# SwiGLU's result turned by VectorE's block transposes and GpSimd's moves instead of TensorE's transposes, in 13 of 22 blocks

## The chip, the cores and the metric

The kernel runs on one core of one Trainium2 chip. Its time is the device time of one execution in microseconds (us); runs before and after are compared by their medians. Where a row comes from a profile, it is from one profiled execution.

## What is computed

One decoder layer for 256 tokens (`SEQ`) of width 2048: a SwiGLU feed-forward layer (half step), a token mixer, and a second SwiGLU layer, each between two RMS norms and with shift, scale and gate from a conditioning vector `c`. The part that matters here:

```python
def swiglu(h, w_gate, w_up, w_down):
    return (jax.nn.silu(h @ w_gate) * (h @ w_up)) @ w_down

mod = (jax.nn.silu(c) @ w_ada[l] + b_ada[l]).reshape(b_, N_SUBLAYERS, N_MOD, D_MODEL)
x = sublayer(x, 0, ffn(0), 0.5)
x = sublayer(x, 1, mixer, 1.0)
x = sublayer(x, 2, ffn(1), 0.5)
```

`D_FF` is 5632. All inputs are float32, and all weights are read once.

## The kernel before

**Weights.** A weight tile is 256 rows by 512 columns, 512 KB. SyncE's queue (SP) issues one load for it into a buffer of the pool `raw`, which has 8 buffers of 4 KB a partition (L304). ScalarE (ACT) rounds it to `wh` (L315), VectorE (DVE) subtracts to get the rest `wl` (L320), each in one of `NW = 4` buffers, and TensorE (PE) multiplies three times for each product: `wh` with the activation's high part (L338), `wl` with it (L339), `wh` with its low part (L340). A tile takes 12 such multiplications of 512 columns. Loads go out in order; each waits for its buffer, which is free when the subtraction has read the tile that was in it.

**The conditioning vector.** Its products with `w_ada` are made by DVE alone, from buffers of the same pool `raw` (loads L157 and L162, sums L170 and L172). These "side" units are spread between the weight tiles: many in the first feed-forward layer, few in the second.

**Blocks.** The feed-forward width is cut into 11 blocks of 512 for each layer. A block makes gate and up in PSUM, tokens on partitions (`proj_tok`); `swiglu_evac` or `swiglu_sum` makes silu(gate) * up as two tiles `gt` of 128 tokens by 512. The down product needs the result with the feed-forward width on partitions. `to_g` does that: for each half of the block four transposes by TensorE (L542) into one PSUM bank, then `split_act`, which rounds on ACT (L373) and subtracts on DVE (L374) into the slot `g`. Blocks are grouped in "supers": after the gates and ups of a super its down products run. In layer 0 the supers have 4, 4 and 3 blocks (the blocks of the first have parts of the work done earlier), in layer 1 they have 4, 4 and 3.

**Order.** The evacuation is a generator in the list `pending`; after every weight tile `pump` lets it go one step. `swiglu_evac` takes its first step behind the first weight tile of the next block; both halves of `to_g` come two and three tiles later. `flush` runs what is left at the end of a block. The order of instructions on each engine, and which buffer of a pool a tile gets, are settled when the kernel is compiled.

Of the kernel before, what the change touches and what calls it, by code (L numbers as in the profile page):

```python
# [8 lines left out]
F32 = mybir.dt.float32  # L9
# [5 lines left out]
P = 128  # L15
D = 2048
S = 256
NT = S // P
# [14 lines left out]
def tile_layer(  # L33
# [6 lines left out]
    nc = tc.nc  # L40
# [14 lines left out]
    rawp = ctx.enter_context(tc.tile_pool(name="rawp", bufs=8))  # L55
# [9 lines left out]
    def nm(s):  # L65
        uid[0] += 1
        return f"{s}_{uid[0]}"

    def ps():
        return psp.tile([P, 512], F32, tag="ps", name=nm("ps"))  # L70

    def t2(shape=(P, 512), dtype=F32):
        return tp.tile(list(shape), dtype, tag="t2", name=nm("t2"))
# [203 lines left out]
    pending = []  # L277
# [17 lines left out]
    def flush():  # L295
        while pending:
            pump()
# [39 lines left out]
    def mm3(o, lh, ll, rh, rl, start, stop):  # L337
        nc.tensor.matmul(o, lh, rh, start=start, stop=False, skip_group_check=True)  # L338
        nc.tensor.matmul(o, lh, rl, start=False, stop=False, skip_group_check=True)  # L339
        nc.tensor.matmul(o, ll, rh, start=False, stop=stop, skip_group_check=True)  # L340

    def hold(src, segs, c0, nw):

        n = sum(nk for _, nk, _ in segs) // 2
        slots = [Slot((P, 2, 2, 512), F32R) for _ in range(n - nw)]
        return list(w_tiles(src, segs, c0, [None] * min(n, nw) + [s_.t for s_ in slots])), slots
# [14 lines left out]
    def proj_tok(src, c0, begun=None, w=512, segs=FULL, banks=None, first=0):  # L361

        if begun is not None:
            banks, segs = begun[0], FULL[begun[1]:]
        banks = banks or [ps(), ps()]
        last = segs[-1][0] + segs[-1][1] - 1
        for k, wh, wl in w_tiles(src, segs, c0, w=w):
            for t in range(NT):
                tok_mm(k, wh, wl, t, banks[t][:, 0:w], first, last)
        return banks  # L370

    def split_act(dh, dl, src):
        act = nc.scalar.copy(dh, src)  # L373
        return nc.vector.tensor_tensor(out=dl, in0=src, in1=dh.bitcast(F32), op=ALU.subtract), act  # L374


    def parts():

        p = small((P, 8), "parts")
        nc.gpsimd.memset(p[:, 3:4], EPS)  # L380
        return p

    def sumsq(p, q, src):
        junk = t2()
        nc.scalar.activation(junk, src, AF.Square, scale=float(D) ** -0.5, accum_out=p[:, q + q // 3:q + q // 3 + 1])  # L385
# [147 lines left out]
        return banks, 2  # L533


    def to_g(g, gts):
        for i in range(2):
            pg = ps()
            for j in range(2):
                for t in range(NT):  # L540
                    m = 2 * i + j
                    nc.tensor.transpose(pg[:, j * S + t * P:j * S + (t + 1) * P], gts[t][:, m * P:(m + 1) * P], ident)  # L542
            split_act(g.t[:, 0, 2 * i:2 * i + 2, :], g.t[:, 1, 2 * i:2 * i + 2, :],
                      pg.rearrange("p (k s) -> p k s", s=S))
            yield

    def swiglu_evac(g, gb, ub):
        gts = []
        for t in range(NT):
            sg, gt = t2(), t2()  # L550
            nc.scalar.activation(sg, gb[t], AF.Silu)
            nc.vector.tensor_tensor(out=gt, in0=sg, in1=ub[t], op=ALU.mult)
            gts.append(gt)
        yield
        yield
        yield from to_g(g, gts)

    def swiglu_sum(gb, ub, part):

        pv = part.t.rearrange("p k s -> p (k s)")  # L560
        gts = []
        for t in range(NT):
            sg, gt = t2(), t2()
            nc.vector.tensor_tensor(out=sg, in0=pv[:, t * 512:(t + 1) * 512], in1=gb[t], op=ALU.add)
            nc.scalar.activation(sg, sg, AF.Silu)
            nc.vector.tensor_tensor(out=gt, in0=pv[:, 1024 + t * 512:1024 + (t + 1) * 512], in1=ub[t], op=ALU.add)
            nc.vector.tensor_tensor(out=gt, in0=sg, in1=gt, op=ALU.mult)
            gts.append(gt)
        part.free()
        g = Slot((P, 2, 4, S), F32R)  # L570

        def rest():
            yield
            yield
            yield from to_g(g, gts)

        pending.append(rest())
        return g

    def ffn(idx, supers, begun, xin, nxt, nxt_src=None, nxt_c0=None, nxt_w=512):  # L580

        y = None
        yp = [parts() for _ in range(NT)]

        def evac_y(si, q, t, bank):
            ys = y[t].t[:, q * 512:(q + 1) * 512]
            if si == 0:
                nc.scalar.copy(ys, bank)
            else:
                nc.vector.tensor_tensor(out=ys, in0=ys, in1=bank, op=ALU.add)  # L590
            if si == len(supers) - 1:
                sumsq(yp[t], q, ys)

        for si, blocks in enumerate(supers):
            gs = []
            n = len(blocks)
            for b, segs, part, banks in blocks:
                if si == 0 and begun is not None and not gs:
                    gb = proj_tok(w_ff_gate[idx], b * FB, begun)
                    ub = proj_tok(w_ff_up[idx], b * FB)  # L600
                elif part is not None:
                    gb = proj_tok(w_ff_gate[idx], b * FB, segs=segs, first=segs[0][0])
                    ub = proj_tok(w_ff_up[idx], b * FB, segs=segs, first=segs[0][0])
                    flush()
                    gs.append(swiglu_sum(gb, ub, part))
                    continue
                else:
                    gb = proj_tok(w_ff_gate[idx], b * FB, segs=segs, banks=banks and banks[0])
                    ub = proj_tok(w_ff_up[idx], b * FB, segs=segs, banks=banks and banks[1])
                flush()  # L610
                gs.append(Slot((P, 2, 4, S), F32R))
                pending.append(swiglu_evac(gs[-1], gb, ub))
            if y is None:
                y = [Slot((P, D)) for _ in range(NT)] if xin[0].__class__ is Half else [Half(t) for t in range(NT)]
            rows = [(4 * i, 4, 4 * b[0]) for i, b in enumerate(blocks)]

            def mms(k, wh, wl, t):
                g = gs[k // 4].t
                mm3(banks[t], g[:, 0, k % 4, t * P:(t + 1) * P], g[:, 1, k % 4, t * P:(t + 1) * P],
                    wh, wl, k == 0, k == 4 * n - 1)  # L620

            for q in range(4):
                banks = [ps(), ps()]
                if si == len(supers) - 1 and q == 2:
                    for s_ in xin:
                        s_.t
                if si == len(supers) - 1 and q == 3:
                    flush()
                    if side[0] is not None:
                        side[0].drain()  # L630
                    early = early_w(nxt_src, nxt_c0, nxt_w)
                    kept, slots = hold(w_ff_down[idx], rows, q * 512, NW if nxt is None else 3)

                    def last_mm(t):
                        for k, wh, wl in kept:
                            mms(k, wh, wl, t)

                    return boundary(last_mm, lambda t: evac_y(si, q, t, banks[t]), lambda t: times_gg(y, t, q), xin, y, yp, slots + gs,
                                    early, 1, nxt, nxt_src, nxt_c0, nxt_w)
                else:  # L640
                    for k, wh, wl in w_tiles(w_ff_down[idx], rows, q * 512):
                        for t in range(NT):
                            mms(k, wh, wl, t)
                    for t in range(NT):
                        later(evac_y, si, q, t, banks[t])
                        if si == len(supers) - 1:
                            later(times_gg, y, t, q)
            if si < len(supers) - 1:
                for g in gs:
                    g.free()  # L650
# [68 lines left out]
    for bs, n in (((0, 1, 2, 3, 4), 1), ((5, 6), 2), ((7,), 3)):  # L719
        first.until(n - 1)  # L720
        for b in bs:
            part = Slot((P, 8, S))
# [5 lines left out]
    banks = [proj_tok(gate_up[u], 8 * FB, segs=FULL[:3]) for u in range(2)]  # L728
# [26 lines left out]
    blocks = [(4718, 410), (4308, 410), (3896, 412), (3484, 412), (G0, 412)]  # L755
# [61 lines left out]
    for i, (c0, w) in enumerate(blocks):  # L817
        banks = proj_tok(w_in, c0, begun if i == 0 else None, w)
# [147 lines left out]
    for i in range(2):  # L966
        banks = proj_t(w_in, i * 512)
# [72 lines left out]
    for i in range(2):  # L1040
        banks = proj_tok(w_in, O0 + i * 512)
# [44 lines left out]
    for q in range(4):  # L1086
        banks = b0 if q == 0 else [ps(), ps()]
# [55 lines left out]
```

## Time and profile before

| what | us |
|---|---|
| median of 3 runs | 1872.24 |
| lowest and highest | 1871.8 and 1872.76 |
| the profiled execution | 1872.83 |
| its span, first to last instruction | 1870.8 |

The profiled execution is 0.6 us above the median; 2.0 us of it lie outside its span. In the rows, PE is TensorE, PEld its weight loads, POOL is GpSimd, SPq is SyncE's queue. L followed by a number is a line of the kernel. A row of a group gives the count, the busy time and the mean of one instruction; what stands behind the last bar is the idle time just before them and who ended it. Shapes are partitions x elements.

### The profile page before, as it was taken

To read this page: it belongs to the slowest core of one execution; us is meant where nothing else is said; L and a number is where in the kernel's file an instruction comes from. 1 tells how busy PE (TensorE), PEld (TensorE's weight loads), DVE (VectorE), ACT (ScalarE), POOL (GpSimd) and SP (SyncE) were. 2 spreads that over 40 slices of the span, in tenths; PEclk is the share of its full clock that TensorE was granted. 3 is DMA by queue.
4 is the path that set the end of the run, shared out by engine and by line. 5 is a ranking of instruction groups with operands and counts; after the bars stand their busy time and mean duration, and the time that the engine had idled before them with its cause. 6 is when DMAs were issued, how large, how long until landed. Compare 5 with 4: busy or idle time off the path is not lost.

```text
span 1870.8 us, 23057 instructions
## 1 busy us (share of the span) xinstructions
PE 1823.0 (97%) x8501; PEld 1523.7 (81%) x8501; DVE 1365.0 (73%) x1479; ACT 853.6 (46%) x1058; POOL 22.5 (1%) x42
## 2 busy tenths in 40 slices
PE   3999999999999999999999999999999999999998
PEld 2888888888888888799988887888888888888886
DVE  6888798788987888868898987555556555556455
ACT  3555444444443444655545446444444444334443
POOL 1000000000000000000000000000000000000000
PEclk9999999999999999999999999999999999999999
DMA  9999889999899999578689994776677776677662
GB/s 346 346 359 342 314 293 318 319 307 322 294 331 323 340 306 334 188 240 278 218 288 306 358 342 141 221 223 213 228 228 221 221 223 214 219 228 220 190 190 91
DMA packets 232617, 499.82 MB, mean 267 GB/s; under 512 B 16828, under 2 KB 28332, under 8 KB 231992
## 3 DMA queue, kind: packets, MB, share of 16 engines
q1 hardware_dynamic: 232504, 498.36, 79.9%
q8 instruction: 66, 1.08, 0.2%
q14 instruction: 47, 0.39, 0.1%
HBM read 496.19 MB, written 2.10 MB: 266 GB/s over the span
## 4 chain that ended last, share of the span: by engine, by line
PE 86%; issue 8%; DVE 3%; DMA 2%; POOL 1%; ACT 0%; DVEq 0%; POOLq 0%; ACTq 0%; SPq 0%
PE ps L338 28%; PE ps L339 28%; PE ps L340 28%; DVE acc L172 2%; PE ps L542 1%; DVE wl L320 1%; DMA raw<-in_w_ada_dram 1%; DMA raw<-in_w_ff_up_dram 0%; POOL rstd L391 0%; DMA raw<-in_w_ff_gate_dram 0%; DMA xt<-in_x_dram 0%; PE ps L197 0%; PE ps L930 0%; ACT wh L315 0%; POOL brs L808 0%
## 5 line engine op out<-in xcount | busy, mean ns | idle before, releaser
L320 DVE TENSOR_TENSOR wl<-raw,wh 128x1024 fp32r<-128x1024 f32 (+2 forms) x635 | 766.1, 1210 | 450.3 <-ACT wh L315 449.3
L315 ACT CAST wh<-raw 128x1024 fp32r<-128x1024 f32 (+2 forms) x637 | 662.6, 1043 | 864.1 <-PE ps L340 737.0
L338 PE MATMUL ps<-wh,hh 128*128 128x512 f32 (+2 forms) x1680 | 650.3, 390 | 1.5 <-ACT hh L373 1.5
L339 PE MATMUL ps<-wl,hh 128*128 128x512 f32 (+2 forms) x1680 | 649.3, 387 | 1.2 <-DVE wl L320 1.2
L340 PE MATMUL ps<-wh,hl 128*128 128x512 f32 (+2 forms) x1680 | 649.1, 386 | 0.0
L339 PEld LDWEIGHTS ps<-wl,hh 128*128 128x128 f32 x1680 | 316.5, 188 | 61.9 <-DVE wl L320 2.7
L340 PEld LDWEIGHTS ps<-wh,hl 128*128 128x128 f32 x1680 | 316.1, 188 | 60.5
L338 PEld LDWEIGHTS ps<-wh,hh 128*128 128x128 f32 x1680 | 315.9, 188 | 60.1 <-ACT hh L373 1.7
L172 DVE SCALAR_TENSOR_TENSOR acc<-raw,cs,acc 128x1024 f32<-128x1024 f32 x270 | 345.1, 1278 | 0.8 <-DVE parts L389 0.4
L338 PE MATMUL ps<-wh,big 128*128 128x512 f32 x804 | 314.6, 392 | 0.0
L339 PE MATMUL ps<-wl,big 128*128 128x512 f32 x804 | 313.1, 389 | 0.2 <-DVE wl L320 0.2
L340 PE MATMUL ps<-wh,big 128*128 128x512 f32 x804 | 313.1, 389 | 0.0
L339 PEld LDWEIGHTS ps<-wl,big 128*128 128x128 f32 x804 | 151.0, 188 | 31.8 <-DVE wl L320 1.0
L340 PEld LDWEIGHTS ps<-wh,big 128*128 128x128 f32 x804 | 150.9, 188 | 31.7
L338 PEld LDWEIGHTS ps<-wh,big 128*128 128x128 f32 x804 | 150.9, 188 | 30.6
L338 PE MATMUL ps<-hh,wh 128*128 128x256 f32 x128 | 37.6, 293 | 0.0
L680 ACT COPY big<-ps 128x512 f32<-128x512 f32 x32 | 18.7, 589 | 40.8 <-PE ps L340 39.5
L374 DVE TENSOR_TENSOR big<-ps,big 128x512 fp32r<-128x512 f32 x52 | 35.5, 683 | 1.3 <-ACT big L373 1.2
L340 PE MATMUL ps<-hh,wl 128*128 128x256 f32 x128 | 36.2, 283 | 0.0
L339 PE MATMUL ps<-hl,wh 128*128 128x256 f32 x128 | 36.2, 283 | 0.0
L373 ACT CAST big<-ps 128x512 fp32r<-128x512 f32 x52 | 30.1, 578 | 0.0
L385 ACT ACTIVATE t<-xt 128x512 f32<-128x512 f32 x32 | 20.0, 626 | 17.7 <-DVE xt L590 9.6
(194 smaller groups left out, 751.4 us busy)
## 6 DMA issues: line engine op xcount, KB each, us to landing
raw<-in_w_ada_dram SPq DMA_DIRECT2D x224, 512.0 KB, 5.3
raw<-in_w_ff_gate_dram SPq DMA_DIRECT2D x176, 512.0 KB, 4.5
raw<-in_w_ff_up_dram SPq DMA_DIRECT2D x176, 512.0 KB, 4.5
raw<-in_w_ff_down_dram SPq DMA_DIRECT2D x176, 512.0 KB, 5.1
raw<-in_w_ada_dram SPq DMA_DIRECT2D x128, 256.0 KB, 5.5
raw<-in_w_in_dram SPq DMA_DIRECT2D x48, 512.0 KB, 5.1
raw<-in_w_out_dram SPq DMA_DIRECT2D x32, 512.0 KB
raw<-in_w_in_dram SPq DMA_DIRECT2D x24, 412.0 KB, 4.8
```

The source lines that it names most:

```text
L172: ins = nc.vector.scalar_tensor_tensor(a, raw[:, j, :, :], cs[:, k:k + 1], a, op0=ALU.mult, op1=ALU.add)
L315: behind(nc.scalar.copy(wh, rawv), floor[1])
L320: last_split[0] = nc.vector.tensor_tensor(out=wl, in0=rawv, in1=wh.bitcast(F32), op=ALU.subtract)
L338: nc.tensor.matmul(o, lh, rh, start=start, stop=False, skip_group_check=True)
L339: nc.tensor.matmul(o, lh, rl, start=False, stop=False, skip_group_check=True)
L340: nc.tensor.matmul(o, ll, rh, start=False, stop=stop, skip_group_check=True)
L373: act = nc.scalar.copy(dh, src)
L374: return nc.vector.tensor_tensor(out=dl, in0=src, in1=dh.bitcast(F32), op=ALU.subtract), act
L385: nc.scalar.activation(junk, src, AF.Square, scale=float(D) ** -0.5, accum_out=p[:, q + q // 3:q + q // 3 + 1])
L542: nc.tensor.transpose(pg[:, j * S + t * P:j * S + (t + 1) * P], gts[t][:, m * P:(m + 1) * P], ident)
L680: nc.scalar.copy(part.t.rearrange("p k s -> p (k s)")[:, u * 1024 + i * 512:u * 1024 + (i + 1) * 512], banks[i])
```

## The change

A block takes another way than `to_g` where the next block of its super still multiplies at least 12 of the 16 groups of 128 weight rows, which is 12 to 16 weight tiles for gate and up. These are 3 and 2 blocks of the last two supers of layer 0 and 3, 3 and 2 of layer 1: 13 of 22. In that way VectorE transposes each `gt` in blocks of 32 by 32 into `tr`, GpSimd copies 16 pieces (32 partitions by 256 elements, in runs of 32) to their places in `gf`, and nine weight tiles later `split_act` reads `gf` instead of PSUM. `tr` and `gf` are tiles of the pool `raw`. The other nine blocks go on as before.

```diff
+    def to_g_blocks(g, gts):
+        tr = rawp.tile([P, NT, 4, 4, 32], F32, tag="raw", name=nm("tr"))
+        gf = rawp.tile([P, 4, NT, 4, 32], F32, tag="raw", name=nm("gf"))
+        for t in range(NT):
+            nc.vector.transpose(tr[:, t].rearrange("p m q r -> p (m q r)"), gts[t])
+        for b in range(4):
+            for q in range(4):
+                nc.gpsimd.tensor_copy(gf[q * 32:(q + 1) * 32, :, :, b, :].rearrange("p m t r -> p t m r"),
+                                      tr[b * 32:(b + 1) * 32, :, :, q, :])
+        for _ in range(9):
+            yield
+        for i in range(2):
+            split_act(g.t[:, 0, 2 * i:2 * i + 2, :], g.t[:, 1, 2 * i:2 * i + 2, :],
+                      gf[:, 2 * i:2 * i + 2].rearrange("p m t b r -> p m (t b r)"))
+            yield
...
-    def swiglu_evac(g, gb, ub):
+    def swiglu_evac(g, gb, ub, blocks):
...
         yield
-        yield
-        yield from to_g(g, gts)
-
-    def swiglu_sum(gb, ub, part):
+        if blocks:
+            yield from to_g_blocks(g, gts)
+        else:
+            yield
+            yield from to_g(g, gts)
+
+    def swiglu_sum(gb, ub, part, blocks):
...
         def rest():
             yield
-            yield
-            yield from to_g(g, gts)
+            if blocks:
+                yield from to_g_blocks(g, gts)
+            else:
+                yield
+                yield from to_g(g, gts)
...
-            for b, segs, part, banks in blocks:
+            for i, (b, segs, part, banks) in enumerate(blocks):
+
+                slow = i + 1 < n and sum(nk for _, nk, _ in blocks[i + 1][1]) >= 12
```

## Rows read from the trace of the kernel before

**Rows 1.** The page's first part: busy time, share, instructions of each engine.
```profile
PE 1823.0 (97%) x8501; PEld 1523.7 (81%) x8501; DVE 1365.0 (73%) x1479; ACT 853.6 (46%) x1058; POOL 22.5 (1%) x42
```

**Rows 2.** The page's chain that ended last, shares of the span by line.
```profile
PE ps L338 28%; PE ps L339 28%; PE ps L340 28%; DVE acc L172 2%; PE ps L542 1%; DVE wl L320 1%; DMA raw<-in_w_ada_dram 1%; DMA raw<-in_w_ff_up_dram 0%; POOL rstd L391 0%; DMA raw<-in_w_ff_gate_dram 0%; DMA xt<-in_x_dram 0%; PE ps L197 0%; PE ps L930 0%; ACT wh L315 0%; POOL brs L808 0%
```

**Rows 3.** Waits over the whole span: us in total, times, longest.
```profile
ACT wh L315 <- PE ps L340: 737.0, 460, 3.2
DVE wl L320 <- ACT wh L315: 449.3, 418, 3.8
```

**Rows 4.** Stretches: busy us (instructions) of PE, PEld, DVE, ACT, POOL; clock, DMA share, GB/s.
```profile
405.00:507.00 102.00, 102.00 (x475) 83.94 (x474) 90.04 (x97) 44.12 (x48) 0.00 (x0) 1.00 0.90 310
630.00:720.00 90.00, 90.00 (x413) 74.23 (x412) 73.12 (x69) 38.48 (x41) 0.00 (x0) 1.00 0.93 321
1165.00:1340.00 175.00, 175.00 (x789) 144.85 (x788) 98.12 (x89) 74.91 (x81) 0.00 (x0) 1.00 0.71 221
```

**Rows 5.** Timeline of PE in layer 1: start us, us, instruction.
```profile
1179.73 0.39 PE L338 MATMUL ps<-wh,hh 128*128 128x512 f32 x1
...
1182.45 0.39 PE L338 MATMUL ps<-wh,hh 128*128 128x512 f32 x1
...
1183.13 0.60 PE L542 MATMUL ps<-ident,t 128*128 128x128 f32 x4
...
1186.34 0.60 PE L542 MATMUL ps<-ident,t 128*128 128x128 f32 x4
```

**Rows 6.** Groups by line and shape: DVE's, then ACT's.
```profile
L320 DVE TENSOR_TENSOR wl<-raw,wh 128x1024 fp32r<-128x1024 f32 x597 | 728.0, 1222 | 431.8 <-ACT wh L315 430.9 <-issue 0.3
...
L374 DVE TENSOR_TENSOR big<-ps,big 128x512 fp32r<-128x512 f32 x52 | 35.5, 683 | 1.3 <-ACT big L373 1.2
...
L183 DVE STREAM_TRANSPOSE t<-acc 128x512 f32<-128x512 f32 x22 | 14.6, 692 | 0.1
...
L374 DVE TENSOR_TENSOR hl<-t,hh 128x512 fp32r<-128x512 f32 x14 | 9.3, 686 | 0.1
...
L315 ACT CAST wh<-raw 128x1024 fp32r<-128x1024 f32 x599 | 629.3, 1054 | 829.2 <-PE ps L340 707.0 <-issue 35.6 <-DMA raw<-in_w_ff_gate_dram 26.4
L373 ACT CAST big<-ps 128x512 fp32r<-128x512 f32 x52 | 30.1, 578 | 0.0
...
L373 ACT CAST hh<-t 128x512 fp32r<-128x512 f32 x14 | 8.3, 620 | 0.1
```

**Rows 7.** POOL's groups by line and shape; the last gives min/median/max ns.
```profile
L318 POOL TENSOR_TENSOR wl<-raw,wh 128x1024 fp32r<-128x1024 f32 x2 | 4.7, 2358 | 22.2 <-ACT wh L315 17.8 <-DMA raw<-in_w_ada_dram 4.4
...
L380 POOL MEMSET parts<- 128x1 f32 x12 | 1.1, 98 | 0.6
...
L843 POOL TENSOR_SCALAR_AFFINE_SELECT big<-onesr 128x128 f32<-128x128 f32 x1 | 0.3, 292 | 1.1 <-PE ps L340 1.1
masks.py:197 POOL MEMSET ident<- 128x128 f32 x1 | 0.2, 204 | 0.3 <-POOLq L1130 0.3
...
L391 POOL TENSOR_TENSOR rstd<-parts,nhalf x12: 548/548/1534, 11.2 to 1864.0; 128x1 f32<-128x1 f32 x12
```

**Rows 8.** Timelines of POOL and DVE in the mixer: start us, us, instruction.
```profile
895.75 1.18 POOL L891 TENSOR_SCALAR_AFFINE_SELECT t<-t 128x512 f32<-128x512 f32 x1 [43.31 <-DMA raw<-in_w_in_dram]
907.81 0.64 POOL L891 TENSOR_SCALAR_AFFINE_SELECT t<-t 128x512 f32<-128x512 f32 x1 [10.88 <-DMA raw<-in_w_in_dram]
...
895.74 0.68 DVE L898 TENSOR_TENSOR t<-t,t 128x512 f32<-128x512 f32 x1
...
907.94 1.05 DVE L898 TENSOR_TENSOR t<-t,t 128x512 f32<-128x512 f32 x1
```

**Rows 9.** Timelines of DVE and PE in layer 0: one tile's subtraction, its first use.
```profile
403.68 1.22 DVE L320 TENSOR_TENSOR wl<-raw,wh 128x1024 fp32r<-128x1024 f32 x1
...
408.61 0.40 PE L339 MATMUL ps<-wl,hh 128*128 128x512 f32 x1
```

**Rows 10.** Line L304's loads, 405 to 507 us: issue to landing.
```profile
DMA to landing us min/median/max: 4.3/5.3/6.8
```

More of the change, by code (lines that the diff above doesn't have):

```diff
@@ L604, in ffn @@
                     flush()
-                    gs.append(swiglu_sum(gb, ub, part))
+                    gs.append(swiglu_sum(gb, ub, part, slow))
                     continue
@@ L611, in ffn @@
                 gs.append(Slot((P, 2, 4, S), F32R))
-                pending.append(swiglu_evac(gs[-1], gb, ub))
+                pending.append(swiglu_evac(gs[-1], gb, ub, slow))
             if y is None:
```

## The prediction, made blind

> **What bounds the kernel now.** I read the busy shares first: TensorE is busy 97% of the span, VectorE 73%, ACT 46%, GpSimd 1% [rows 1]. The chain that ended last runs through TensorE's three products with 28% each, and the transposes L542 have 1% of it by themselves [rows 2]. The waits turn it round: ACT's rounding waits for TensorE 460 times, to get a `wh` buffer back, and VectorE's subtraction waits for ACT [rows 3]. So the splitting of weights runs ahead of TensorE and is held by it; what shortens TensorE's own row of work shortens the kernel, as long as VectorE, the loads and the buffers keep ahead.
>
> How far ahead differs by stage, so I read three stretches [rows 4]: 405 to 507 us (three of the changed blocks, layer 0), 630 to 720 us (two, layer 0) and 1165 to 1340 us (layer 1, which has eight). TensorE is busy throughout in all three. VectorE is busy 90.0 of 102 us in the first, 73.1 of 90 in the second, 98.1 of 175 in the third. The loads move 310, 321 and 221 GB/s. Layer 1 has much room, the first stretch little.
>
> **What the change removes.** In layer 1 a tile without transposes takes TensorE 1182.45 - 1179.73 = 2.72 us from one of its instructions to the same one a tile later; a tile with four transposes in front takes 1186.34 - 1183.13 = 3.21 us [rows 5]. A group of four costs 0.49 us, a block's two groups 0.98 us, 13 blocks 12.7 us. This is work on the engine that sets the end, so it comes off whole if nothing else gets late.
>
> **What it adds on VectorE and ACT.** Two transposes of 128x512 a block. The same shape stands in the rows at 692 ns [rows 6], where pairs overlap a little; I take 1.3 us a block. The rounding and the subtraction read SBUF in place of PSUM: 620 for 578 ns and 686 for 683 ns [rows 6], nothing for two of each. They come nine tiles later (24.5 us), and the down product that reads `g` comes after the super's last block, so nobody waits for them. ACT is under half busy in all stretches [rows 4].
>
> **What it adds on GpSimd.** 16 moves a block, 32 partitions by 256 elements; the trace shows no such move. One-input work there is the select: 292 ns for 128 elements [rows 7], 0.64 us for 512 when nothing is in its way [rows 8]. Between them lies 0.41 us for 256. Below stands the memset, which reads nothing: 98 ns for 1 and 204 ns for 128 elements [rows 7], so 0.31 us. Above stand the 0.55 us that one element costs in the power and the 2358/1024 = 2.3 ns an element of two-input work [rows 7], together 1.14 us. A move reads one input and writes one output as the select does; I take 0.41 us, 6.6 us a block.
>
> **What the moves do to VectorE.** Rows 8 are the ones to look at. At 907.81 a select starts first and takes 0.64; VectorE's two-input instruction starting at 907.94 takes 1.05 us, where its like takes 0.68, and ends only after the select did. At 895.74 VectorE starts first, and the select takes 1.18 us, so it waited. [...] A move thus costs VectorE up to its own length.
>
> In layer 1 a tile of 2.72 us leaves 1.5 us beside the subtraction, room for three moves: 16 take some 5.3 tiles, and the split comes after nine. A block of 16 tiles lasts 16 x 2.72 + 0.98 = 44.5 us, then 43.5; VectorE rises from 56% of it, 24.9 us [rows 4], to 24.9 + 1.3 + 6.6 = 32.8, about 75%. A tile's split also has slack: with four `wh` buffers a tile is wanted three tiles after its rounding starts, 3 x 2.72 - 1.05 - 1.22 = 5.9 us after its subtraction ends [rows 6]. I cost the moves at nothing here; the cover is those 1.5 us a tile and the 5.9 us. Layer 1 keeps 8 x 0.98 = 7.8 us.
>
> In the first stretch, layer 0, the cover is thin. Without the transposes it lasts 102 - 2.9 = 99.1 us. VectorE's work is 90.0 + 3 x 1.3 = 93.9, so 5.2 us are free. Three blocks of moves are 19.7 us. With VectorE idle only 12% of the time most of them push an instruction aside; between all and half I take three quarters, 14.8 us. That is 9.6 too much. The tightest subtraction there ends at 404.90 and is first used at 408.61 [rows 9], so 3.7 us of lateness are free, and TensorE waits 5.9 us (10.8 if all the moves push, 1.0 if half do). With 0.31 us a move it waits 2.3. In the second stretch 88.0 - 73.1 - 2.6 = 12.3 us are free and the moves take 9.8: no wait.
>
> [...]
>
> **Buffers and loads.** `tr` and `gf` take two of eight `raw` buffers, the first until the last move, the second until the late split. At 310 GB/s a 0.524 MB tile goes by every 1.69 us, so eight buffers turn in 13.5 us and six in 10.1. A tile needs 5.3 to land [rows 10], 1.05 and 1.22 for its split [rows 6]: 7.6. It fits by 2.5 us; in layer 1, at 221 GB/s, by 6.6. I cost it at nothing; what covers it is that gap, and rival three is what happens without it.
>
> **The sum.** 1872.83 (the profiled execution, 0.6 above the median) - 12.7 + 5.9 = 1866.0 us.
>
> **Rivals.**
> *One, all of it is hidden* (0.20): VectorE keeps its turn and the moves slip into its pauses. [...] Then 12.7 us come off whole: 1860.1. For it: GpSimd is idle otherwise [rows 1]. Against it: in rows 8 VectorE does wait.
>
> *Two, the moves are long* (0.14): at 1.14 us each the first stretch is short by 0.75 x 54.7 - 5.2 - 3.7 = 32 us, the second by 0.75 x 36.5 - 12.3 - 3.7 = 11, and in layer 1 the moves need 18.2 us where 1.5 of 2.72 are free, 33 us, 8.5 more than nine tiles; less 5.9 this is 2.6 a block, 21 in all. 1872.8 - 12.7 + 64 = 1924. It decides from 0.60 us a move, where 0.75 x 48 x 0.60 - 8.9 eats 12.7; from 0.70 the kernel is slower. For it: runs of only 32 elements, which no row has. Against it: the select's price.
> [...]
>
> *Three, the loads get stuck behind `tr`* (0.10), also on the slower side: loads go out in order, each into the buffer fixed for it. If a move only gets in after each VectorE instruction, 16 of them take 16 x (1.22 + 0.41) = 26 us, where a buffer turns in 13.5; the load that is due in `tr`'s buffer, and all behind it, are 12.6 us late. 2.5 + 5.9 of that are covered, 4.2 remain, in five blocks 21: 1872.8 - 12.7 + 21 = 1881. It decides from 2.5 us a block. For it: the loads at 0.90 share [rows 4]. Against it: it needs the buffer to come up that early.
>
> **Chances and range.** My forecast has 0.46, with a range of 1861 to 1871 by its own bounds; the rivals 0.20, 0.14 and 0.10; 0.10 is left for a mixture near no change or for another order of instructions than I think. 0.2% is 3.7 us, about what a measurement tells from no change. Faster by more: rival one, the forecast but for its upper end, and a little of the rest, 0.60. Within: 0.16. Slower: rivals two and three in most of their weight and some of the rest, 0.24. The range goes from 1859, just under rival one, to 1882, just over rival three; left out is most of rival two.
>
> **What would show it.** After the change L542 should count 72 instead of 176. DVE transposes should rise by 26, POOL should show 208 copies near 0.4 us, longer where VectorE was first. In layer 1 TensorE should have no new waits, and blocks should be 0.98 us shorter. In the first stretch TensorE should wait for `wl` by some 6 us, VectorE be busy nearly all the time. I am wrong if POOL's copies run beside the subtraction with neither slower, if a copy alone takes over 0.6 us, or if waits of ACT for loads appear in layer 0.

## The result, and the profile after

The changed kernel takes 1979.92 us (median of 4 runs), the kernel before 1872.02 beside it: the ratio is 1.0573, with a 95% interval of 1.056 to 1.0587. I had forecast 1866 and a range up to 1882. It is slower by 107.9 us.

The page of the changed kernel, its first part; then the rows of its groups by line and shape that answer to [rows 6, 7], and the moves' line by itself (min/median/max ns):
```profile
PE 1851.3 (94%) x8397; PEld 1533.3 (78%) x8397; DVE 1378.1 (70%) x1505; ACT 850.3 (43%) x1058; POOL 118.8 (6%) x250
```
```profile
L374 DVE TENSOR_TENSOR big<-gf,big 128x512 fp32r<-128x512 f32 x26 | 16.9, 688 | 88.4 <-ACT big L373 88.4
L542 DVE STREAM_TRANSPOSE tr<-t 128x512 f32<-128x512 f32 x26 | 17.0, 689 | 0.0
...
L545 POOL COPY gf<-tr x208: 390/394/1302, 402.6 to 1862.0; 32x256 f32<-32x256 f32 x104
```
The durations are as forecast: a move takes 0.39 us by itself, a transpose 0.69, and TensorE has 104 transposes fewer. VectorE's and ACT's busy shares have fallen. TensorE's idle time has grown by 79 us, from 47.8 (1870.8 - 1823.0) to 126.8 (1978.1 - 1851.3), so most of the loss went into waits; but its busy time has grown too, by 28 us, though it has less to do. The sections behind the experiments come back to that. The waits over the whole span (us in total, times, longest), of all engines, then TensorE's, then those of SyncE's queue:
```profile
ACT wh L315 <- PE ps L340: 618.4, 386, 3.6
...
ACT big L373 <- POOL gf L545: 151.8, 13, 14.8
```
```profile
PE ps L338 <- ACT wh L315: 71.8, 13, 9.3
...
PE ps L339 <- DVE wl L320: 8.2, 17, 1.6
```
```profile
SPq L304 <- POOL gf L545: 95.0, 12, 8.8
...
SPq L304 <- DVE tr L542: 45.8, 10, 6.9
...
SPq L157 <- POOL gf L545: 7.9, 1, 7.9
...
SPq L157 <- DVE tr L542: 4.7, 1, 4.7
```
Two queues wait for the moves. ACT's rounding of `gf` does so in each of the 13 blocks, for 151.8 us together, and the queue of the loads does so 13 times too, for 102.9 us. That queue waits another 50.5 us for the transposes that write `tr`, in 11 of the 13 blocks: there its next load stood before the moves had begun. TensorE then waits 71.8 us for rounded weights, once a block; the kernel before has no such wait.

One block of layer 1 shows the order of things. The timelines of POOL, ACT, SPq and DVE of the changed kernel, around 1230 us:
```profile
1229.66 7.78 POOL L545 COPY gf<-tr 32x256 f32<-32x256 f32 x16 [43.83 <-DVE tr L542]
1280.56 7.78 POOL L545 COPY gf<-tr 32x256 f32<-32x256 f32 x16 [43.12 <-DVE tr L542]
```
```profile
1224.84 1.05 ACT L315 CAST wh<-raw 128x1024 fp32r<-128x1024 f32 x1 [1.18 <-PE ps L340]
1237.46 1.14 ACT L373 CAST big<-gf 128x512 fp32r<-128x512 f32 x2 [11.57 <-POOL gf L545]
1238.51 3.88 ACT L315 CAST wh<-raw 128x1024 fp32r<-128x1024 f32 x4
```
```profile
1208.27 16.56 SPq L304 DMA_DIRECT2D raw<-in_w_ff_gate_dram  x6
1237.46 0.34 SPq L157 DMA_DIRECT2D raw<-in_w_ada_dram  x1
```
```profile
1228.24 1.30 DVE L542 STREAM_TRANSPOSE tr<-t 128x512 f32<-128x512 f32 x2
1229.46 1.18 DVE L320 TENSOR_TENSOR wl<-raw,wh 128x1024 fp32r<-128x1024 f32 x1
1238.12 1.29 DVE L374 TENSOR_TENSOR big<-gf,big 128x512 fp32r<-128x512 f32 x2 [7.47 <-ACT big L373]
```
The transposes end at 1229.54 and the last move at 1237.44. ACT's next instruction after 1225.89 is already the rounding of `gf`, not nine tiles later but one weight rounding behind the block's last silu. It waits 11.57 us, and four weight roundings that follow are done right behind it. In the same moment, at 1237.46, the next load goes out, 12.6 us after the one before it: 4.7 us of that it waited for the transposes, then 7.9 for the moves. From block to block it is 50.9 us (1280.56 - 1229.66), where I had reckoned with 43.5.

Stretches of this block (busy us and instructions of PE, PEld, DVE, ACT, POOL; granted clock, DMA share, GB/s):
```profile
1230.00:1234.00 4.00, 4.00 (x20) 3.30 (x19) 0.64 (x1) 0.00 (x0) 3.67 (x9) 1.00 0.00 0
...
1236.00:1238.00 2.00, 0.00 (x0) 0.00 (x0) 0.00 (x0) 0.54 (x2) 1.31 (x4) 1.00 0.00 0
1238.00:1240.00 2.00, 0.40 (x1) 0.29 (x1) 1.71 (x3) 2.00 (x4) 0.00 (x0) 0.65 0.67 160
1240.00:1242.00 2.00, 1.53 (x4) 0.94 (x4) 2.00 (x3) 2.00 (x3) 0.00 (x0) 0.50 1.05 401
1242.00:1244.00 2.00, 2.00 (x6) 1.53 (x5) 2.00 (x2) 0.39 (x1) 0.00 (x0) 0.50 1.00 367
```
The loads have stopped altogether (DMA share 0.00) while only GpSimd and TensorE work; then TensorE runs dry; and when it goes on, its granted clock is 0.50.

### The profile page after: what moved, and what is told of

It is laid out like the page before. It is cut to its first block, busy times and chain, and to the rows that moved or that the text cites. A ratio compares the mean times of both kernels' runs of the same rounds, so it can differ in the third digit from the quotient of the medians.

```text
span 1978.1 us, 23114 instructions
## 1 busy us (share of the span) xinstructions
PE 1851.3 (94%) x8397; PEld 1533.3 (78%) x8397; DVE 1378.1 (70%) x1505; ACT 850.3 (43%) x1058; POOL 118.8 (6%) x250
## 5 line engine op out<-in xcount | busy, mean ns | idle before, releaser
L338 PE MATMUL ps<-wh,hh 128*128 128x512 f32 (+2 forms) x1680 | 658.5, 397 | 73.3 <-ACT wh L315 71.8
L339 PE MATMUL ps<-wl,hh 128*128 128x512 f32 (+2 forms) x1680 | 664.1, 395 | 8.2 <-DVE wl L320 8.1
L340 PE MATMUL ps<-wh,hl 128*128 128x512 f32 (+2 forms) x1680 | 660.1, 393 | 0.0
L338 PEld LDWEIGHTS ps<-wh,hh 128*128 128x128 f32 x1680 | 323.7, 193 | 140.6 <-ACT wh L315 77.3
L339 PEld LDWEIGHTS ps<-wl,hh 128*128 128x128 f32 x1680 | 323.3, 192 | 80.8 <-DVE wl L320 18.7
L340 PEld LDWEIGHTS ps<-wh,hl 128*128 128x128 f32 x1680 | 323.2, 192 | 61.4
L545 POOL COPY gf<-tr 32x256 f32<-32x256 f32 x208 | 96.2, 463 | 1260.2 <-DVE tr L542 1209.0
L373 ACT CAST big<-gf 128x512 fp32r<-128x512 f32 x26 | 14.8, 615 | 151.8 <-POOL gf L545 151.8
L374 DVE TENSOR_TENSOR big<-gf,big 128x512 fp32r<-128x512 f32 x26 | 16.9, 688 | 88.4 <-ACT big L373 88.4
L570 DVE TENSOR_TENSOR t<-t,ps 128x512 f32<-128x512 f32 x28 | 18.8, 685 | 25.0 <-PE ps L340 24.5
```

The costliest lines, as they stand in the source:

```text
L545: nc.gpsimd.tensor_copy(gf[q * 32:(q + 1) * 32, :, :, b, :].rearrange("p m t r -> p t m r"), tr[b * 32:(b + 1) * 32, :, :, q, :])
```

## The experiments

Three theories went in. **Order:** the nine idle steps don't put the split off; its rounding waits in ACT's queue for the moves, and the weights wait behind it. **Port:** the moves hold VectorE's subtractions back. **Buffers:** two raw buffers less, or loads that stand behind the moves.

### held: the split can't move forward in ACT's queue

```diff
+        last_cast[0] = nc.scalar.copy(wh, rawv)      # in split_w
...
+            _, act = split_act(...)                  # in to_g_blocks
+            behind(act, last_cast[0])
```


> The changed kernel, with one thing more: the rounding of gf on ACT is ordered behind the newest weight rounding at the point where it stands in the program, so it can't move forward in ACT's queue. Theory of the order (in the changed kernel the rounding of gf stands one weight rounding behind the transposes in ACT's queue, waits there for all 16 moves, and the weights behind it wait too): the waits of ACT for the moves vanish, the time is that of before less 12.7 us plus the few us that layer 0 gives back, 1860 to 1868. Theory of the port (the moves hold VectorE's subtractions back): little comes back, over 1940. Theory of the buffers (two raw buffers less stop the loads): tr and gf are held as long or longer, over 1940.

Measured 1945.66 us, ratio 1.0387 (1.0371 to 1.0402). ACT no longer waits for the moves, yet only 34 us came back. So the theory of the order is at most a part of it; the number fits the theory of the port and that of the buffers alike. The waits of SyncE's queue between 1215 and 1262 us, and its timeline there beside POOL's:
```profile
SPq L158 <- POOL gf L547: 12.4, 1, 12.4
SPq L158 <- DVE tr L544: 4.7, 1, 4.7
```
```profile
1227.99 12.30 POOL L547 COPY gf<-tr 32x256 f32<-32x256 f32 x16 [43.84 <-DVE tr L544]
...
1240.32 0.34 SPq L158 DMA_DIRECT2D raw<-in_w_ada_dram  x1
1240.76 0.38 SPq L305 DMA_DIRECT2D raw<-in_w_ff_gate_dram  x1
1241.23 2.64 SPq L305 DMA_DIRECT2D raw<-in_w_ff_up_dram  x5
```
A load of the side unit goes out at 1240.32, 0.03 us after the last move ends at 1240.29, and six more behind it at once. It had waited first for the transposes that write `tr`, then for the moves that read it, 17.1 us together: that is the load due in `tr`'s buffer. The six that followed at once had buffers that were free, and had stood behind it.

### one_yield: one idle step in place of nine

```diff
-        for _ in range(9):
+        for _ in range(1):
```


> The changed kernel with one idle step in place of nine between moves and split. Theory of the order: the idle steps don't set the place in ACT's queue, so nothing changes: 1975 to 1985, the same 13 waits of ACT for the moves, some 150 us. If the nine steps do put the split off, it comes earlier now and waits longer: over 2000. Theory of the buffers: gf is given back earlier, so it is faster than 1960.

A single run took 1977.46 us, as the theory of the order says; ACT waits for the moves 13 times here too, 147.5 us in all. In the compiled order the rounding of `gf` stands at the same place, one weight rounding behind the evacuation, with nine steps and with one. So the steps set a place in the program and not in ACT's queue. Why the compiled order puts it there is not shown; it may have reckoned the moves to be done by then.

### beside and raw6: the moves alone, the buffers alone

```diff
 beside (on the changed kernel; gf is read by nobody):
-        for _ in range(9):
-            yield
-        for i in range(2):
-            split_act(..., gf[:, 2 * i:2 * i + 2]...)
-            yield
+        yield
+        yield from to_g(g, gts)
 raw6 (on the kernel before):
-    rawp = ctx.enter_context(tc.tile_pool(name="rawp", bufs=8))
+    rawp = ctx.enter_context(tc.tile_pool(name="rawp", bufs=6))
```


> The kernel before, with the 26 transposes and 208 moves of the change added, into tr and gf, which nobody reads; the outcome still goes by TensorE and PSUM. Theory of the order: nobody waits for the moves, so they cost what they push aside on VectorE and in the buffers, 1870 to 1880. Theory of the port: VectorE is held back as in the changed kernel, over 1940. Theory of the buffers: gf is given back right behind the moves, so a part of the loss, 1900 to 1940.

> The kernel before with six raw buffers in place of eight all the time. Theory of the order: my reckoning holds that a tile needs 7.6 us where six buffers turn in 10.1, so no loss in layer 1 and little in layer 0, 1871 to 1878. Theory of the buffers: a loss as in the changed kernel, over 1940.

Measured: beside 1941.87 us, 1.0371 (1.0354 to 1.0389); raw6 1896.39 us, 1.0122 (1.0107 to 1.0137). So moves that nobody reads cost 69 us, as the theory of the port says in its number and the theory of the order does not; the range of the theory of the buffers is missed by 2 us. But the waits of SyncE's queue in beside name the loads, not VectorE:
```profile
SPq L304 <- POOL gf L545: 178.7, 12, 18.6
```
The loads wait 178.7 us for the moves, and 16.2 more in a wait of L157. And six buffers cost 23 us, over my upper end, so my reckoning was wrong there too; but not in layer 1. A stretch of raw6 there, then GpSimd's last power ahead of layer 1, in raw6 and in the kernel before:
```profile
1220.00:1410.00 190.00, 190.00 (x851) 157.36 (x850) 104.17 (x92) 82.14 (x87) 0.00 (x0) 1.00 0.68 220
```
```profile
1156.47 0.55 POOL L391 TENSOR_TENSOR rstd<-parts,nhalf 128x1 f32<-128x1 f32 x1 [6.22 <-DVE parts L389]
```
```profile
1132.79 0.55 POOL L391 TENSOR_TENSOR rstd<-parts,nhalf 128x1 f32<-128x1 f32 x1 [6.01 <-DVE parts L389]
```
TensorE is busy throughout, and the 23 us are all there before layer 1 begins. So two missing buffers by themselves don't stop layer 1. That the reason is one buffer that is due and comes late is put to the test below, in tr_raw and gf_raw.

### held_slot, slot and beside_slot: tr and gf away from the loads

```diff
-        tr = rawp.tile([P, NT, 4, 4, 32], F32, tag="raw", name=nm("tr"))
-        gf = rawp.tile([P, 4, NT, 4, 32], F32, tag="raw", name=nm("gf"))
+        mv = Slot((P, 2, 1024))
+        tr = mv.t[:, 0, :].rearrange("p (t m q r) -> p t m q r", t=NT, m=4, q=4)
+        gf = mv.t[:, 1, :].rearrange("p (m t b r) -> p m t b r", m=4, t=NT, b=4)
```
The slot is freed behind the split (in beside_slot behind the moves).

> The held kernel with tr and gf in an 8 KB slot of another pool (one of the nine that the results g are in), so that no load of weights waits for the moves; all eight raw buffers stay with the loads. Theory of the two queues (in the held kernel SP's next load goes into the buffer of tr and waits for the last move, 17 us without a load; in the changed kernel ACT's queue waits for the same move besides): both waits are gone, so the transposes' 12.7 us come off less what layer 0 gives back by VectorE, 1860 to 1868. Theory of the port: the moves still hold VectorE in layer 0, where it is busy 88%: 1875 to 1900.

> The changed kernel with tr and gf in the slot, the split not held. Theory of the two queues: loads go on, but ACT's queue still waits for the last move, some 11 us a block, of which TensorE's lead covers 5.9, and TensorE's clock falls after its wait: 1930 to 1975. If the loads were the whole loss: 1860 to 1870.

> The kernel before with transposes and moves added that nobody reads, in the slot in place of raw buffers. Nobody waits for the moves and no load stands behind them, so what is left is the price of the moves on VectorE (and of 26 transposes). Theory of the two queues: 1872 to 1876, near nothing. Theory of the port: over 1885.

Measured: held_slot 1859.95 us, 0.9931 (0.9917 to 0.9944), faster than both kernels; slot 1880.22 us, 1.0039 (1.0025 to 1.0052); beside_slot 1872.78 us, 1.0 (0.9991 to 1.0009).

With the loads free of the moves, and ACT all but free (it waits for them four times, 13.8 us in all, which TensorE doesn't feel), the whole 12.7 us come off: 1872.8 - 1859.95 = 12.9. The theory of the port falls with beside_slot, where all moves and transposes run beside the unchanged work and cost nothing that can be measured. Its stretches, the same as in [rows 4]:
```profile
405.00:507.00 102.00, 102.00 (x475) 83.92 (x475) 96.32 (x102) 44.26 (x49) 45.58 (x48) 1.00 0.89 313
630.00:720.00 90.00, 90.00 (x412) 74.29 (x411) 78.38 (x74) 38.38 (x41) 32.84 (x32) 1.00 0.94 330
```
VectorE rises from 90.0 to 96.3 us in the first. Six transposes are 3.9 of it, so 48 moves cost it 2.4 us, 0.05 each; 32 in the second cost 2.7, 0.08 each. A stretch's edge can shift by one instruction of over 1 us; over the whole span VectorE rises by 22.6 us (1387.6 for 1365.0), of which the 26 transposes are 17.3, so 208 moves cost it 5.3 us, 0.03 each. It is GpSimd that pays. In held_slot, the moves' line and one block's moves in layer 0 and layer 1 each; then VectorE beside the latter:
```profile
L548 POOL COPY big<-big x208: 390/765/1455, 405.0 to 1753.4; 32x256 f32<-32x256 f32 x104
...
438.96 18.55 POOL L548 COPY big<-big 32x256 f32<-32x256 f32 x16 [15.87 <-DVE big L545]
...
1215.90 12.36 POOL L548 COPY big<-big 32x256 f32<-32x256 f32 x16 [30.81 <-DVE big L545]
```
```profile
1215.76 1.18 DVE L322 TENSOR_TENSOR wl<-raw,wh 128x1024 fp32r<-128x1024 f32 x1
1216.86 1.42 DVE L173 SCALAR_TENSOR_TENSOR acc<-raw,cs,acc 128x1024 f32<-128x1024 f32 x1
1218.20 1.41 DVE L322 TENSOR_TENSOR wl<-raw,wh 128x1024 fp32r<-128x1024 f32 x1
1220.36 1.47 DVE L322 TENSOR_TENSOR wl<-raw,wh 128x1024 fp32r<-128x1024 f32 x1 [0.75 <-ACT wh L316]
```
A subtraction beside moves takes 1.4 in place of 1.22 us. A move, 0.39 us alone, takes 0.77 at the median, and 16 of them take up to 18.6 us in layer 0 and 12.4 in this block of layer 1 (14.9 at most there).

Slot misses its expectation on the good side. ACT does wait there, in total, times, longest:
```profile
ACT big L373 <- POOL big L546: 93.0, 13, 12.0
```
But the loads went on meanwhile, so ACT found landed tiles behind the wait, and TensorE's lead covered most: ACT's queue alone costs 1880.2 - 1860.0 = 20 us.

### tr_raw, gf_raw and held5_slot: which tile, and how late

```diff
 tr_raw (on held_slot):
+        tr = rawp.tile([P, NT, 4, 4, 32], F32, tag="raw", name=nm("tr"))
 gf_raw (on held_slot):
+        gf = rawp.tile([P, 4, NT, 4, 32], F32, tag="raw", name=nm("gf"))
 held5_slot (on held_slot):
-        for _ in range(9):
+        for _ in range(5):
```


> The held kernel with gf alone in the slot; tr stays in a raw buffer, which is free again behind the last move. Theory of the load stuck behind tr: one load in order waits for the last move in every block, so most of the held kernel's loss stays, 1925 to 1946. Theory of fewer buffers: seven of eight buffers left, so at most half of its loss stays, under 1910.

> The held kernel with tr alone in the slot; gf stays in a raw buffer, which it has from the first move until behind the late split, longer than tr's. Theory of the load stuck behind tr: the buffer of gf is given back by VectorE in the order of the weight tiles, so no load waits out of order; seven buffers cost a few us in layer 0 at most, 1860 to 1868. Theory of fewer buffers: at least as slow as with tr in a raw buffer, over 1890.

> The kernel with the split held and both tiles in the slot, with five idle steps in place of nine. The moves take 12.5 us in layer 1 and up to 18.5 us in layer 0 there, 4.6 and 6.8 tiles, and TensorE's lead is 5.9 us. Theory of the two queues: the split stands behind enough tiles in layer 1, and in layer 0 its wait is covered by the lead: 1859 to 1864. If the wait in layer 0 shows on TensorE: 1864 to 1875.

Measured: tr_raw 1927.82 us, 1.0295 (1.028 to 1.0311); gf_raw 1866.46 us, 0.9968 (0.9956 to 0.9979); held5_slot 1874.51 us, 1.0009 (1.0 to 1.0019).

The first two lie within the ranges of the theory of the load stuck behind `tr`. Each of them has seven raw buffers left for the loads. `tr`, which holds its buffer for the shorter time, costs 68 us over held_slot; `gf`, which holds it longest, 6.5. In tr_raw SyncE's queue waits for the moves, in total, times, longest:
```profile
SPq L305 <- POOL big L548: 99.9, 8, 14.1
SPq L158 <- DVE acc L173: 69.6, 70, 3.2
SPq L158 <- POOL big L548: 65.9, 5, 13.3
```
That is 13 waits, one a block. In gf_raw there is no such wait. So most of the loss is the load that waits for the last move, and not the number of buffers.

With five steps the split is held at its place in the program, but that place is too early for layer 0. ACT waits for the moves in every block again, and TensorE's 102 us between 405 and 507 are no longer full, while the stretch in layer 1 is:
```profile
ACT big L375 <- POOL big L548: 74.8, 13, 10.3
```
```profile
405.00:507.00 102.00, 95.11 (x416) 75.74 (x415) 84.58 (x91) 38.88 (x44) 33.96 (x48) 0.98 0.80 274
...
1165.00:1340.00 175.00, 175.00 (x778) 144.89 (x777) 102.61 (x96) 75.67 (x82) 32.42 (x48) 1.00 0.72 224
```
It gives back 14.6 us, all that the change brings; the expectation's second case holds, at its far end. A reason that I only argue: ACT runs some three tiles ahead of TensorE, so five tiles of its queue are less time than I had counted.

## Why the prediction was wrong

**What bounds the kernel, and the transposes: right.** TensorE's transposes came off at their price, 12.9 us measured in held_slot for 12.7.

**Durations: right.** Transposes 689 for 692 ns, the split's halves 615 and 688 for 620 and 686, a move 0.39 for 0.41 us. A move's eight runs of 32 elements thus cost no more than the select's rate. Rival two falls with that. Beside VectorE's work a move took 0.77 us at the median in held_slot, over the 0.60 from which that rival was to decide, and still nothing was lost.

**"They come nine tiles later, and nobody waits for them": this step failed.** I took the steps of the program for places in ACT's queue. The rounding stood one weight rounding behind, waited for all 16 moves in every block (151.8 us), and held the weights; nine steps or one made no difference. Nobody waits for `g` itself, that much was right; but the weight roundings that stand behind the split in ACT's queue waited with it: 11.57 us in the block at 1230 us, with four of them right behind.

**"I cost it at nothing" (buffers and loads): this step failed too, and is the larger one.** I asked whether six buffers are enough on average. In layer 1 they are, as raw6 shows; ahead of it even that was wrong, by 23 us. What decided was rival three: the load due in `tr`'s buffer waits for the last move, and the queue behind it. I gave it 0.10 and 21 us, in layer 0 alone. It came up in all 13 blocks, layer 1's included, and `tr` in a raw buffer costs 68 us with all else in order. The way into it was another than mine: I had the moves last 26 us, but in the changed kernel they last 7.7 to 8.7 us a block, and in most blocks the load stands there from before the transposes end. I had argued against it that the buffer must come up so early; a buffer that is given to the moves comes up in its turn like any other. The sign that I had named came too: between 380 and 790 us, in layer 0, ACT waits 26.7 us for loads of gate, up and down weights, where it waited 4.0 before.

**The two together.** Against before, with order as changed or held and tiles in raw buffers or in the slot: +108, +73, +7, -13 us. ACT's wait alone costs 20 us, and tiles in raw buffers alone 86 (`tr`'s 68 and `gf`'s 6.5 among them); both together cost 121, more than their sum. Why they add up to more is not shown; both end with the same last move. Where the time stands can be read from held_slot's page, beside the changed kernel's above:
```profile
PE 1809.6 (97%) x8397; PEld 1512.9 (81%) x8397; DVE 1388.3 (75%) x1505; ACT 852.5 (46%) x1058; POOL 201.4 (11%) x250
```
Of the 120 us between the two spans (1978.1 and 1858.2), TensorE is idle for 78; the waits of 71.8 + 8.2 us above hold nearly all of that. For the other 42 it is busy longer (1851.3 for 1809.6 us) with the same 8397 instructions, at a mean granted clock of 0.972 for 0.999. The last section shows one such stretch.

**VectorE held back by the moves: mis-sized.** The term of 5.9 us was an estimate: from the two selects of [rows 8] I let a move cost VectorE up to its own length, and I chose a share of three quarters. No run shows that term. In beside_slot it measured 0 (1872.78 us for 1872.80), and in the stretches of layer 0 a move takes 0.05 to 0.08 us from VectorE, not 0.31. Instructions of both engines get longer beside each other, but mostly the moves do: in held_slot 0.77 us at the median for 0.39 alone, a subtraction 1.4 for 1.22. In the kernel as changed the term could hardly show: in the block above VectorE had one subtraction beside the moves and then no more weights to split.

## What to carry to other kernels

A delay written as steps of a generator is no delay in an engine's queue (nine steps 1979.92 us, one 1977.46): where the compiled order decides, tie a late reader of a slow engine's output behind an instruction of its own queue, and look at the compiled order, not at the program. Don't lend a buffer from a ring of loads where a slow engine gives it back late: the load due in that buffer stops all loads behind it, though other buffers are free (`tr`, 68 us). `gf`, which an instruction in the order of the weight tiles gives back, cost 6.5. And price a wait by the queue behind it, not by the average need of buffers.

## What the runs showed of the hardware that was not expected

TensorE's granted clock fell after a wait, from 1.00 to 0.50. In the changed kernel TensorE's last product ahead of the gap began at 1235.30, and the next at 1239.60, after an idle time of 3.92 us; from 1240 to 1244 the granted clock is 0.50, and products follow each other at 0.43 us:
```profile
1235.30 0.39 PE L340 MATMUL ps<-wh,hl 128*128 128x512 f32 x1
1239.60 0.79 PE L338 MATMUL ps<-wh,hh 128*128 128x512 f32 x1 [3.92 <-ACT wh L315]
...
1241.45 0.63 PE L340 MATMUL ps<-wh,hl 128*128 128x512 f32 x1
1241.88 0.63 PE L338 MATMUL ps<-wh,hh 128*128 128x512 f32 x1
...
1245.59 0.40 PE L338 MATMUL ps<-wh,hh 128*128 128x512 f32 x1
1245.82 0.40 PE L339 MATMUL ps<-wl,hh 128*128 128x512 f32 x1
```
They followed each other at 0.23 us before and again from 1245.59 on. Some ten products at 0.43 in place of 0.23 us are by estimate 2 us, so this wait cost some 2 us more than the 3.92 that it lasted. That the 42 us by which TensorE is busy longer than in held_slot are all of this kind is inferred from the mean clock; the rows show it for one block. And where GpSimd's moves and VectorE's subtractions ran at the same time, in held_slot, they got longer unevenly: a move took twice its time (0.77 us at the median for 0.39), a subtraction a sixth more (1.4 for 1.22).
